# W behind four rows of x on the sync queue, the small loads alone on the scalar queue, and six transpositions of the identity at PE's start

## Chip, cores, metric

One core of one Trainium2 chip. The metric is the device time in microseconds of one execution (the slowest core, here the only one). The profile's span runs from the first to the last instruction and is about 1.3 us shorter than the time of the same execution. In the views PE, PEld (weight loads), DVE, ACT, POOL and SP are the engines, a q behind a name is that engine's sequencer, and `L213` is line 213 of the kernel.

## The reference

```python
x: [16, 2048, 256] f32 -> x_flat [32768, 256];  W: [256, 256];  lora_A: [256, 16];  lora_B: [16, 256];  lora_E: [16]
y = x_flat @ W + scale * (((x_flat @ lora_A) * lora_E) @ lora_B)
```

The kernel folds the low-rank part into the weights once: `weff = W + (A * E * scale) @ B`, and then does one product, `x_flat @ weff`. It must read 33.6 MB of x and write 33.6 MB of y.

## The kernel before

x is cut in 8 chunks of 4 MB. Six of them have a home in SBUF at a time; y is written over x in the same home, and a store sends it out. For each group of four rows per partition, POOL casts x to bf16 (`stage`), PE transposes it, ACT copies the result (`xt`), PE multiplies by `weff`, and DVE copies the product into the home. The parts that the argument touches:

```python
ROWS = 32; N_CHUNKS = 8; N_HOMES = 6
LOAD_PIECES = {0: [8, 8, 16]}            # chunk 0 is loaded in three pieces, the others in one of 4 MB
ORDER = ["L0", "L1", "L2", "L3", "L4", "L5",
         "S0", "S1", "L6", "L7", "S2", "S3", "S4", "S5", "S6", "S7"]
EARLY_AFTER = 1
HELD = N_HOMES - 1
...
    def sync_program():
        def load(pc):
            c, s, e = pc
            if c == N_HOMES - 1:
                sync.wait_ge(s_weff, 1)            # home 5 holds W until weff is made
            if c >= N_HOMES:
                sync.wait_ge(stored_of[c - N_HOMES], 16)
            ...
        opening.append(load(pieces[0]).ins.name)   # issued ahead of the entry barrier
        for step in ORDER:
            ...
                if c == EARLY_AFTER:               # the loads of chunk 2 and on wait for the first output
                    sync.wait_ge(s_first, 1)
                    sync.dma_start(out=y_chunks[0, :16, 0, :32], in_=home(0)[:16, 0, :32]).then_inc(s_early, 16)
            else:
                sync.wait_ge(s_chunk, c + 1)
                ...
                sync.dma_start(out=y_chunks[c], in_=home(c)[:]).then_inc(...)
...
    def gpsimd_program():
        ...
            if (c, b) == (HELD, 0):                # chunk 5 is not begun before stores 0 and 1 have landed
                for held_by in stored_of.values():
                    gpsimd.wait_ge(held_by, 16)
...
    def tensor_program():
        ...
        tensor.wait_ge(s_ident, 2)
        tensor.wait_ge(set_up_loaded["a"], 16)
        for t in range(KT):
            ins = tensor.transpose(psum_y[0][:R, t, :P], a_sb[:, t, :], ident[:])
        ...
        turn(0)
        ...   # (A*E)^T @ B
        turn(1)
        with tensor.Fori(0, N_GROUPS // UNROLL):
            for i in range(UNROLL):
                turn(i + 2)
                multiply(i)                        # so three groups are turned before the first product
```

## Time and profile before

| | before |
|---|---|
| time, median | 162.81 us (three runs, 162.21 to 162.82; with a fourth, 162.69) |
| span | 160.5 us (of a profiled execution of 161.79 us) |
| bytes moved | 67.43 MB |
| sync queue's packets, share of 16 DMA engines | 97.9% |
| last DVE copy ends / last store issued | 122.0 / 122.1 us |

The page of the kernel before, the 40-slice view (one digit is the busy tenths of a 4 us slice):

```profile
PE   0585979999999999400019999999990000000000
...
DVE  0102796999999999700003799899993000000000
...
DMA  7999999999999999999999999999999999999993
GB/s 262 432 425 466 449 393 425 490 392 408 498 400 392 492 400 400 400 417 466 425 400 451 457 392 433 474 402 425 466 400 433 466 408 433 449 425 417 441 449 155
```

and its DMA queues (packets, MB, share of 16 engines' span; q1 belongs to the sync queue, q10 to the scalar queue):

```profile
q1 hardware_dynamic: 2624, 67.11, 97.9%
q10 hardware_dynamic: 352, 0.30, 0.5%
```

The compute engines are idle for whole stretches; the DMA engines never are. The end of the chain of waits of the kernel before (start us, us, what), and from the view of waits of the sync queue its last wait (total us, times, longest):

```profile
120.74 0.02 issue
120.76 1.22 DVE home L213
```

```profile
SPq L264 <- SPq L264: 36.6, 1, 36.6
```

The chain ends with a DVE copy at 122 us because it follows instructions only. What comes after it is the sync engine waiting 36.6 us for stores that are already queued. That is the first thing to learn from these lines: the last instruction on a compute engine lies 38 us before the end.

The timeline of the kernel before in the head (start us, us, engine line op, names, shapes, count, idle before and what ended it):

```profile
0.00 2.44 SPq L131 DMA_DIRECT2D home<-in_x_dram  x4
...
1.99 0.53 ACTq L185 DMA_DIRECT2D home<-in_W_dram  x1
...
5.11 0.59 PE L248 MATMUL psum_y<-ident,home 128*16 128x128 f32 x2 [5.11 <-DMA home<-in_lora_A_dram]
...
12.95 0.69 DVE L208 TENSOR_TENSOR weff<-home,psum_y 128x512 bf16<-128x512 f32 x1 [5.91 <-DMA home<-in_W_dram]
...
13.79 1.86 PE L236 MATMUL psum_y<-weff,xt 128*128 128x256 bf16 x8 [2.48 <-PEq L221]
...
16.99 0.36 SPq L144 DMA_DIRECT2D out_dram<-home  x1
17.40 1.84 SPq L131 DMA_DIRECT2D home<-in_x_dram  x4
```

Here is what the change is aimed at: `weff` waited 5.9 us for W, and everything after it is late.

### The profile page before, as it was taken

The numbers are of one execution on the slowest core, as the hardware profiler recorded it, in microseconds if no ns is written. First come the engines' busy times: TensorE is split into PE (matmuls) and PEld (weight loads), VectorE is DVE, ScalarE is ACT, GpSimd is POOL, SyncE is SP. The second block draws the span as 40 slices with busy tenths as digits, with TensorE's granted clock in tenths as the row PEclk, the third lists the DMA queues.
The fourth block names the chain that finished last, engine by engine and source line by source line (L and its number), as shares of the span: only waits on it lengthen the run. The fifth ranks groups of instructions, "written<-read, shape, count | busy, mean of one in ns | idle before, by whom it ended". The sixth has DMA issues, their size and how long they took to land. (4 is left out here: it accounts for less than half of the span.)

```text
span 160.5 us, 2160 instructions
## 1 busy us (share of the span) xinstructions
PE 94.2 (59%) x782; PEld 83.9 (52%) x782; DVE 79.5 (50%) x66; ACT 66.0 (41%) x65; POOL 67.0 (42%) x70
## 2 busy tenths in 40 slices
PE   0585979999999999400019999999990000000000
PEld 0354869999999999300017999899990000000000
DVE  0102796999999999700003799899993000000000
ACT  3240667777777777400005577777740000000000
POOL 1542648777777777000045577777700000000000
PEclk9999999999999999955555999999998555555555
DMA  7999999999999999999999999999999999999993
GB/s 262 432 425 466 449 393 425 490 392 408 498 400 392 492 400 400 400 417 466 425 400 451 457 392 433 474 402 425 466 400 433 466 408 433 449 425 417 441 449 155
DMA packets 2979, 67.43 MB, mean 420 GB/s; under 512 B 528, under 2 KB 544, under 8 KB 672
## 3 DMA queue, kind: packets, MB, share of 16 engines
q1 hardware_dynamic: 2624, 67.11, 97.9%
q10 hardware_dynamic: 352, 0.30, 0.5%
q14 instruction: 3, 0.02, 0.0%
HBM read 33.85 MB, written 33.56 MB: 420 GB/s over the span
## 5 line engine op out<-in xcount | busy, mean ns | idle before, releaser
L213 DVE COPY home<-psum_y 128x1024 f32<-128x1024 f32 x64 | 78.3, 1225 | 30.0 <-PE psum_y L236 25.3
L173 POOL CAST stage<-home 128x1024 bf16<-128x1024 f32 x64 | 66.3, 1040 | 47.5 <-PE psum_xt L228 21.4
L193 ACT COPY xt<-psum_xt 128x1024 bf16<-128x1024 bf16 x64 | 64.7, 1012 | 49.8 <-PE psum_xt L228 49.8
L236 PE MATMUL psum_y<-weff,xt 128*128 128x256 bf16 x512 | 69.4, 281 | 2.6 <-PEq L221 2.5
L236 PEld LDWEIGHTS psum_y<-weff,xt 128*128 128x128 bf16 x512 | 51.4, 101 | 9.6 <-issue 3.2
L228 PE MATMUL psum_xt<-ident,stage 128*128 128x128 f32 x264 | 42.5, 287 | 18.6 <-PEq L221 18.6
L228 PEld LDWEIGHTS psum_xt<-ident,stage 128*128 128x128 f32 x264 | 33.1, 149 | 21.1 <-issue 20.2
L198 DVE TENSOR_SCALAR home<-psum_y,e_sb 16x256 f32<-16x256 f32 x1 | 0.5, 472 | 6.6 <-DMA e_sb<-in_lora_E_dram 6.6
L208 DVE TENSOR_TENSOR weff<-home,psum_y 128x512 bf16<-128x512 f32 x1 | 0.7, 689 | 5.9 <-DMA home<-in_W_dram 5.9
L248 PE MATMUL psum_y<-ident,home 128*16 128x128 f32 x2 | 0.6, 394 | 5.1 <-DMA home<-in_lora_A_dram 5.1
L248 PEld LDWEIGHTS psum_y<-ident,home 128*16 128x16 f32 x2 | 0.1, 87 | 5.1 <-issue 5.1
L193 ACT ACT_TABLE_LOAD x1 | 1.3, 1283 | 2.5 <-issue 2.5
L254 PE MATMUL psum_y<-home 16*128 16x256 f32 x4 | 2.1, 670 | 0.2 <-DMA home<-in_lora_B_dram 0.2
L254 PEld LDWEIGHTS psum_y<-home 16*128 16x128 f32 x4 | 1.2, 319 | 0.8 <-DMA home<-in_lora_B_dram 0.6
L152 POOL MEMSET ident<- 128x128 f32 x1 | 0.2, 204 | 0.7 <-SPq L268 0.7
L154 POOL TENSOR_SCALAR_AFFINE_SELECT ident<-ident 128x128 f32<-128x128 f32 x1 | 0.3, 292 | 0.2 <-POOL ident L152 0.2
L290 POOL MEMSET const-float32-0.0<- 128x1 f32 x1 | 0.1, 98 | 0.2 <-issue 0.2
L290 POOL MEMSET const-bfloat16-1.0<- 128x1 bf16 x1 | 0.1, 101 | 0.0
L290 POOL MEMSET const-uint8-127<- 128x1 uint8 x1 | 0.1, 101 | 0.0
L290 POOL MEMSET const-float32-1.0<- 128x1 f32 x1 | 0.1, 98 | 0.0
## 6 DMA issues: line engine op xcount, KB each, us to landing
out_dram<-home SPq DMA_DIRECT2D x8, 4096.0 KB, 39.7
home<-in_x_dram SPq DMA_DIRECT2D x7, 4096.0 KB, 20.8
home<-in_x_dram SPq DMA_DIRECT2D x2, 1024.0 KB, 5.7
home<-in_x_dram SPq DMA_DIRECT2D x1, 2048.0 KB, 11.5
home<-in_W_dram ACTq DMA_DIRECT2D x1, 256.0 KB, 10.9
home<-in_lora_A_dram ACTq DMA_DIRECT2D x1, 16.0 KB, 4.9
e_sb<-in_lora_E_dram ACTq DMA_DIRECT2D x1, 0.1 KB, 5.5
home<-in_lora_B_dram ACTq DMA_DIRECT2D x1, 16.0 KB, 5.8
```

Of the source, the lines that this page charges most:

```text
L152: gpsimd.memset(ident[:], 0.0).then_inc(s_ident, 1)
L154: gpsimd.affine_select(out=ident[:], in_=ident[:], compare_op=ALU.not_equal, fill=1.0, base=0, pattern=[[-1, P]], channel_multiplier=1,).t ...
L173: gpsimd.tensor_copy(out=stage[g % NS][:], in_=home(c)[:, b:b + CG, :]).then_inc(s_stage, 1)
L193: scalar.copy(out=xt[g % NX][:], in_=halves).then_inc(s_xt, 1)
L198: vector.tensor_scalar(out=ate, in0=psum_y[0][:R, :KT, :P], scalar1=e_sb[:], scalar2=float(scale), op0=ALU.mult, op1=ALU.mult,).then_inc(s ...
L208: vector.tensor_add(out=weff[:], in0=w_sb, in1=psum_y[1][:, :KT, :]).then_inc(s_free, NY)
L213: vector.tensor_copy(out=home(c)[:, b:b + CG, :], in_=psum_y[g % NY][:]).then_inc(s_free, 1)
L228: ins = tensor.transpose(psum_xt[i % NT][:, b, :], words[:, b, :], ident[:])
L236: ins = tensor.matmul(psum_y[i % NY][:, b, :], xt[i % NX][:, b, t, :], weff[:, t, :], start=(t == 0), stop=(t == KT - 1),)
L248: ins = tensor.transpose(psum_y[0][:R, t, :P], a_sb[:, t, :], ident[:])
L254: ins = tensor.matmul(psum_y[1][:, t, :], ate[:, t, :], b_sb, start=True, stop=True)
L290: nc = _bacc.Bacc("TRN2", target_bir_lowering=False, num_devices=1)
```

## The change

Intent: bring W early, so that `weff` and the first products come early; keep the scalar queue for the three small loads; let PE do something before A is there, so that its clock is released sooner; spread the early store over three lines.

```diff
-LOAD_PIECES = {0: [8, 8, 16]}
+LOAD_PIECES = {0: [4, 4, 8, 16]}
+WARM_UP = 6
+EARLY_LINES = [5, 6, 7]
...
         opening.append(load(pieces[0]).ins.name)
+        sync.dma_start(out=w_sb, in_=W.rearrange("(q t) m -> q t m", t=KT)).then_inc(set_up_loaded["w"], 16)
...
                     sync.wait_ge(s_first, 1)
-                    sync.dma_start(out=y_chunks[0, :16, 0, :32], in_=home(0)[:16, 0, :32]).then_inc(s_early, 16)
+                    for b, n in enumerate(EARLY_LINES):
+                        sync.dma_start(out=y_chunks[0, :n, b, :32], in_=home(0)[:n, b, :32]).then_inc(s_early, 16)
...
-                    sync.wait_ge(s_early, 16)
+                    sync.wait_ge(s_early, 16 * len(EARLY_LINES))
...
             ("b", b_sb, lora_B),
-            ("w", w_sb, W.rearrange("(q t) m -> q t m", t=KT)),
...
         tensor.wait_ge(s_ident, 2)
+        for i in range(WARM_UP):
+            tensor.transpose(psum_y[1][:, i % CG, :P], ident[:], ident[:])
         tensor.wait_ge(set_up_loaded["a"], 16)
```

## The prediction

> **What bounds it now.** The DMA engines, from first microsecond to last. In the 40-slice view DMA is 9 in every slice but the first (7) and last (3). In the DMA queue view the sync queue's packets fill 97.9% of 16 engines' span, the scalar queue's 0.5%. 67.43 MB move in a 160.5 us span. In the packet records of the trace a 32 KB packet takes 1.213 us (432 GB/s for 16 engines), so the bytes alone cost 156 us. The rest: first packet at 1.0 us, a slow first microsecond, about 0.7 us per engine at 55 to 65 us where loads give way to stores (packets of 1.5 to 1.8 us), and uneven finishing of the engines (158.1 to 160.0 us). PE is busy 59%, DVE 50%. The last DVE copy ends at 122 us (chain of waits), the last store is issued at 122.1, and 38 us of queued stores follow: compute has over 25 us of slack.
>
> **What the change does.**
> 1. W, issued on the scalar queue at 1.99 us, landed 10.9 us later; the weight sum began at 12.95 us after 5.9 us idle (timeline). W now goes out at about 1.1 us on the sync queue behind 512 KB of x, and should land near 4 to 5 us. The sum then waits for the small chain: A landed 5.1, E 6.6, B 7.3, B matmuls ended 9.4. I expect it at 9 to 10.5 us, the first main matmul near 10 (13.8 before).
> 2. Six transpositions of the identity: an estimate from the transposes at 6 us (272 ns each) is 1.6 us, at about 1.9 to 3.6 us, inside PE's wait for A, so free. The first clock record at 1.0 is at 17.4 us. The Trainium skill, "TensorE: Matmul & The Clock Gate", Part 1, says that about 3.4 us of activity releases the clock; six give half of that, so I expect little of them.
> 3. Smaller opening piece: one more issue (0.43 us of the sync queue). The second issue leaves at 1.1 us, its data follow about 1 us later, while the opening piece lasts until about 2.5 us: no DMA gap.
> 4. Three small early stores for one, 18 packets of 128 B for 16, at 13 ns each. The first chunk-2 load is issued at about 14 us, not 17.4; the queue holds work until 21.9, so neither time matters.
>
> **On the critical path: almost nothing.** The bytes are the same and the 16 engines are busy already. The Trainium skill, "DMA: Bandwidth & Descriptors", "Issuing engines are not separate DMA queues", says that queues share the 16 engines; this trace agrees (packets of both queues interleave, total share over 98%). Moving W reorders bytes. The 3 to 4 us won at the head go into slack: chunks 1 to 4 then wait for loads, chunk 5 is held until two stores land at 82 us, and the last store queues as before.
>
> **Predicted: 162.4 us, range 161.4 to 163.4.** Faster by over 2%: 2%; within 2%: 96%; slower by over 2%: 2%.
>
> **What would show it.** Right: DMA share still 97 to 99%, 420 GB/s; span 160 to 161 us; weight sum before 11 us; stores of chunks 0 and 1 landing near 72 and 82 us; last store issued near 122. Wrong: weight sum still waiting for W; a hole in DMA in the first 5 us; A's transposes late; last store issued later.
>
> **What would make it wrong.** If the early small stores change how the first real stores start (the 0.7 us at 58 us), or even out the engines' finish (up to 1.5 us), the time could fall by 1%; a DMA gap after the opening piece could add up to 0.5 us.

## The result and the profile after

| | before | after |
|---|---|---|
| time, median of four runs | 162.69 us (162.21 to 162.82) | 162.97 us (162.79 to 163.05) |
| span of the profile | 160.5 us | 161.6 us |
| `weff` begins | 12.95 us | 8.09 us |
| first product begins | 13.79 us | 11.85 us |
| loads of chunk 2 and on issued from | 17.40 us | 16.17 us |
| last store issued | 122.06 us | 122.78 us |

The ratio is 1.0021, 95% interval 0.9998 to 1.0044. A ratio is the mean time of one kernel's fast runs over that of the other's of the same rounds, so it is not quite the ratio of the medians quoted. The profile of before is of an execution of 161.79 us, quicker than its four timed runs, and that of the changed kernel of the one of 162.91 us: two profiles differ here by 1.1 us where the medians differ by 0.3.

The same views of the changed kernel, 40 slices:

```profile
PE   4858926999999999940009999999990000000000
...
DVE  0114750699999999970003799899993000000000
...
DMA  7999999999999999999999999999999999999993
GB/s 204 386 440 438 454 439 406 454 438 414 446 446 406 446 375 414 422 430 446 430 422 448 414 430 454 406 440 446 397 446 446 406 446 446 406 446 446 414 438 162
```

its DMA queues:

```profile
q1 hardware_dynamic: 2916, 67.37, 98.1%
q10 hardware_dynamic: 208, 0.03, 0.1%
```

the last wait of its sync queue:

```profile
SPq L269 <- SPq L269: 37.0, 1, 37.0
```

and its timeline in the head:

```profile
1.14 0.33 SPq L137 DMA_DIRECT2D home<-in_W_dram  x1
...
1.93 1.54 PE L250 MATMUL psum_y<-ident 128*128 128x128 f32 x6 [1.93 <-POOL ident L158]
...
3.84 0.60 PE L253 MATMUL psum_y<-ident,home 128*16 128x128 f32 x2 [0.37 <-DMA home<-in_lora_A_dram]
...
8.09 0.69 DVE L211 TENSOR_TENSOR weff<-home,psum_y 128x512 bf16<-128x512 f32 x1 [3.06 <-PE psum_y L259]
...
9.79 2.03 POOL L177 CAST stage<-home 128x1024 bf16<-128x1024 f32 x2 [1.45 <-DMA home<-in_x_dram]
...
11.85 1.91 PE L239 MATMUL psum_y<-weff,xt 128*128 128x256 bf16 x8
...
15.10 1.03 SPq L148 DMA_DIRECT2D out_dram<-home  x3
...
16.17 1.79 SPq L133 DMA_DIRECT2D home<-in_x_dram  x4
```

The wait for W is gone, and `weff` is 4.9 us earlier. The first product gains only 1.9 us, the first output 1.9 us, the end nothing. What got worse at the head is the GB/s of the first two slices: 204 and 386 where it was 262 and 432.

The windows view of both kernels for the head. The last two columns matter: share of the 16 DMA engines, and GB/s, both by packets that start in the window.

```profile
0.00:2.00 2.00, 0.00 (x0) 0.00 (x0) 0.00 (x0) 0.00 (x0) 0.70 (x6) 1.00 0.50 111
2.00:5.00 3.00, 0.00 (x0) 0.00 (x0) 0.00 (x0) 1.28 (x1) 0.16 (x1) 1.00 1.01 407
5.00:12.00 7.00, 5.64 (x18) 3.56 (x18) 0.47 (x1) 2.52 (x3) 3.94 (x4) 1.00 1.04 435
```

That is before; this is after:

```profile
0.00:2.00 2.00, 0.07 (x1) 0.08 (x2) 0.00 (x0) 0.01 (x1) 0.70 (x6) 1.00 0.45 82
2.00:5.00 3.00, 2.20 (x9) 1.34 (x10) 0.45 (x1) 1.27 (x1) 1.04 (x1) 1.00 0.97 325
5.00:12.00 7.00, 5.06 (x17) 3.42 (x18) 0.71 (x2) 2.02 (x2) 3.07 (x3) 1.00 1.02 415
```

Between 2 and 5 us the rate falls from 407 to 325 GB/s while the busy share falls by 0.04 only: a few engines stand idle, and some packets take longer than their size asks for. By the packet records 15.1 packets were in flight on the mean from 3 to 5 us (16.4 before; there are 16 engines, and records of one engine overlap a little), and the 4 KB packets of x that start between 2 and 5 us took 0.177 us on the mean, where their median over the whole run is 0.159.

### The profile page after: what moved, and what is told of

The parts are those of the page before. It is cut to its first block, busy times and chain, and to the rows that moved or that the text cites. A ratio compares the mean times of both kernels' runs of the same rounds, so it can differ in the third digit from the quotient of the medians.

```text
span 161.6 us, 2174 instructions
## 1 busy us (share of the span) xinstructions
PE 97.8 (60%) x788; PEld 86.4 (53%) x788; DVE 79.5 (49%) x66; ACT 66.1 (41%) x65; POOL 67.1 (42%) x70
## 3 DMA queue, kind: packets, MB, share of 16 engines
q1 hardware_dynamic: 2916, 67.37, 98.1%
## 5 line engine op out<-in xcount | busy, mean ns | idle before, releaser
L239 PE MATMUL psum_y<-weff,xt 128*128 128x256 bf16 x512 | 70.5, 283 | 0.1
L231 PE MATMUL psum_xt<-ident,stage 128*128 128x128 f32 x264 | 43.6, 292 | 21.3 <-PEq L224 21.3
L239 PEld LDWEIGHTS psum_y<-weff,xt 128*128 128x128 bf16 x512 | 52.1, 102 | 7.1 <-issue 0.3
L231 PEld LDWEIGHTS psum_xt<-ident,stage 128*128 128x128 f32 x264 | 33.7, 152 | 24.4 <-issue 23.6
L250 PE MATMUL psum_y<-ident 128*128 128x128 f32 x6 | 1.5, 430 | 1.9 <-POOL ident L158 1.9
L250 PEld LDWEIGHTS psum_y<-ident 128*128 128x128 f32 x6 | 1.1, 221 | 1.9 <-POOL ident L158 1.9
```

Source lines behind the costliest of these rows:

```text
L231: ins = tensor.transpose(psum_xt[i % NT][:, b, :], words[:, b, :], ident[:])
L239: ins = tensor.matmul(psum_y[i % NY][:, b, :], xt[i % NX][:, b, t, :], weff[:, t, :], start=(t == 0), stop=(t == KT - 1),)
L250: tensor.transpose(psum_y[1][:, i % CG, :P], ident[:], ident[:])
```

## The experiments

Theory S (slack): the DMA engines bound the kernel from start to end, the head is off that path, and its gain vanishes in slack. Beside it, a small loss comes from the pieces of 512 KB at the opening, which feed the DMA engines worse. Rivals: the loss comes from the three early stores or from W's place in the queue, or is noise; or the head does count and a loss elsewhere hides its gain.

Some figures below are worked out from the packet records of the traces. "Moved by 22 us" spreads each packet's bytes evenly over its duration and adds up. "Mean end" is the mean, over the 16 engines, of the start of the last completion packet, and "last end" the latest of them. "Excess" is the time of 32 KB packets above the usual 1.213 us, summed over a stretch and shared out over the 16 engines. Each is from one profile. The kernels of one call ran on one chip: `w_on_sync`, `pieces_only`, `early3_only` and `after_again` (before: median 161.82); `after_8_8_16`, `warm0`, `warm100` and `one_piece` (before: 162.07); `pieces_4x8` and `compute5` (before: 162.12); `warm100_no_gate` and `warm200` (before: 161.84).

| run | chunk 0 in | moved by 12 / 22 us, MB | mean / last end, us | time, median | ratio to before (95%) |
|---|---|---|---|---|---|
| before | 8, 8, 16 | 4.33 / 8.65 | 158.6 / 160.0 | see above | 1 |
| after (first profile) | 4, 4, 8, 16 | 3.94 / 8.27 | 159.6 / 161.2 | 162.97 | 1.0021 (0.9998 to 1.0044) |
| after_again | 4, 4, 8, 16 | 3.98 / 8.30 | 159.4 / 160.8 | 162.77 | 1.0042 (1.0002 to 1.0083) |
| w_on_sync | 8, 8, 16 | 4.22 / 8.55 | 158.7 / 160.5 | 162.01 | 0.9994 (0.9956 to 1.0033) |
| pieces_only | 4, 4, 8, 16 | 3.83 / 8.16 | 159.2 / 161.4 | 162.72 | 1.0023 (0.9981 to 1.0066) |
| early3_only | 8, 8, 16 | 4.05 / 8.38 | 158.8 / 160.0 | 162.29 | 1.0023 (0.9973 to 1.0072) |
| after_8_8_16 | 8, 8, 16 | 4.21 / 8.53 | 158.6 / 159.8 | 162.05 | 0.9993 (0.9968 to 1.0018) |
| warm0 | 4, 4, 8, 16 | 4.01 / 8.33 | 159.4 / 161.0 | 162.76 | 1.0037 (1.0011 to 1.0064) |
| pieces_4x8 | eight of 4 | 3.66 / 7.96 | 159.6 / 160.8 | 163.02 | 1.0054 (1.0023 to 1.0084) |
| one_piece | 32 | 4.32 / 8.63 | 158.5 / 160.5 | 162.59 | 1.0035 (1.0009 to 1.0062) |

One profile has scatter: before and `early3_only` have the same head (the early store comes at 17 us), and yet they differ by 0.27 MB at 22 us. So the groups of runs are compared, and the times decide.

### after_again: is the small loss real?

No edit; the changed kernel with more runs.

> The changed kernel once more, for an interval narrow enough to tell 0.2% from nothing. If the slower head is real: ratio 1.001 to 1.004 with the interval above 1.000; if the first figure was noise: 0.999 to 1.001.

Ratio 1.0042 with an interval just above 1 (1.0002 to 1.0083). By this run alone the loss is barely clear of noise; `warm0` below, which also has the small pieces, adds to it (1.0037, 1.0011 to 1.0064). The loss is about 0.2 to 0.4%.

### w_on_sync: W alone

```diff
+        sync.dma_start(out=w_sb, in_=W.rearrange("(q t) m -> q t m", t=KT)).then_inc(set_up_loaded["w"], 16)
-            ("w", w_sb, W.rearrange("(q t) m -> q t m", t=KT)),
```

> The kernel before with W alone moved to the sync queue (behind eight rows of x; pieces, early store and PE as before). Slack theory: the weight sum moves from 12.95 us to about 9 to 11 us, the time stays within 0.2 us of before (ratio 0.999 to 1.001), DMA share 97 to 99%. Rival (the head counts): 2 to 3 us faster (ratio 0.98 to 0.99). Theory of a slower head: if W's 2 KB packets in the queue of x are what cost the after kernel its 0.3 us, the ratio is about 1.002 and excess packet time or holes show between 2 and 12 us.

`weff` began at 9.43 us, as expected, and the first output was issued at 14.3 us, 2.7 us before the kernel before. The ratio is 0.9994 (0.9956 to 1.0033), which excludes the rival's 0.98 to 0.99: a head that is earlier by 2.7 us is worth nothing that can be seen, and 0.7 us at most. W in x's queue shows no cost either, but the interval would still hide one of the size in question; `after_8_8_16` below narrows that.

### pieces_only: the pieces alone

```diff
-LOAD_PIECES = {0: [8, 8, 16]}
+LOAD_PIECES = {0: [4, 4, 8, 16]}
```

> The kernel before with chunk 0 cut in [4, 4, 8, 16] rows and nothing else. Slack theory with a slower head: most of the 0.3 us loss of the after kernel is here (ratio 1.001 to 1.003), with holes of 0.1 to 0.7 us on some DMA engines between 2 and 5 us after the 512 KB opening piece, since the next piece is issued at 1.1 us and its data come late. Rival (the loss comes from the early stores or is noise): ratio 0.999 to 1.001 and no holes beyond those of before.

Its windows:

```profile
2.00:5.00 3.00, 0.77 (x3) 0.34 (x4) 0.00 (x0) 1.28 (x1) 1.04 (x1) 1.00 0.92 280
```

280 GB/s where before had 407. By the packet records, 12 to 14 packets were in flight between 3 and 5 us, where the kernel before had 16. The holes are there. They are not shared evenly: of the 16 completion updates of the second piece the first came at 4.58 and the last at 7.43 us (in before 7.27 and 7.69), and of those of chunk 1 still at 22.88 and 24.88 (22.30 and 22.77). So some engines fell about 2 us behind the first and stayed behind. One profile has scatter here too: at chunk 1 the spread is 1.0 to 2.0 us in the runs with [4, 4, 8, 16] and 0.5 to 1.2 in those with [8, 8, 16]. The ratio, 1.0023, has an interval that includes 1, so this run alone doesn't settle the time.

### early3_only: the three early stores alone

```diff
-                    sync.dma_start(out=y_chunks[0, :16, 0, :32], in_=home(0)[:16, 0, :32]).then_inc(s_early, 16)
+                    for b, n in enumerate([5, 6, 7]):
+                        sync.dma_start(out=y_chunks[0, :n, b, :32], in_=home(0)[:n, b, :32]).then_inc(s_early, 16)
```

> The kernel before with the one early store of 16 lines replaced by three of 5, 6 and 7 lines. Slack theory with a slower head: no change (ratio 0.999 to 1.001). Rival (the early stores cost time, by putting packets on seven of the 16 engines only or by leaving nine engines without an early store): ratio about 1.002, with the extra time at 55 to 65 us where loads give way to stores, or engines finishing less evenly than 158.1 to 160.0 us.

Ratio 1.0023 (0.9973 to 1.0072): unclear by itself. Nothing of what the rival expected shows in its profile: the excess packet time at 55 to 65 us was smaller than before (0.26 against 0.69 us per engine), and the last end 160.0 us as before. The next run settles the early stores.

### after_8_8_16: everything but the pieces

```diff
-LOAD_PIECES = {0: [4, 4, 8, 16]}
+LOAD_PIECES = {0: [8, 8, 16]}
```

(in the changed kernel)

> The changed kernel with chunk 0 cut in [8, 8, 16] again; W on the sync queue, six transpositions and three early stores stay. If the small pieces are what makes the changed kernel a little slower (holes of the DMA engines at 3 to 5 us, seen with the pieces alone): the rate over the first 5 us goes back from about 225 to about 270 GB/s, packets in flight stay near 16 of 16 engines, and the ratio is 0.998 to 1.002, below that of the changed kernel (1.002 and 1.004). If the early stores or W cost it: ratio stays 1.002 to 1.004.

Its windows:

```profile
2.00:5.00 3.00, 1.46 (x6) 1.06 (x6) 0.00 (x0) 1.27 (x1) 0.13 (x1) 1.00 1.01 381
5.00:12.00 7.00, 6.54 (x23) 4.25 (x24) 1.16 (x2) 2.74 (x3) 3.97 (x4) 1.00 1.04 431
```

The rate is back (381 and 431 GB/s), the mean end is at 158.6 us as before, and the ratio is 0.9993. All six runs (161.63 to 162.32) lie below all six of `warm0` on the same chip (162.43 to 163.15), which has the small pieces (and no transpositions; the changed kernel itself did not run on this chip). W's new place, the transpositions and the early stores together therefore cost nothing visible (the interval ends at 1.0018), and the small loss of the changed kernel is that of the pieces. `pieces_4x8` below, where the pieces alone are changed, says the same. This run even issued its first output earlier than the changed kernel, at 14.29 against 15.10 us (14.46 in the changed kernel's second profile); the reason is under point 1 below.

### warm0: no transpositions of the identity

```diff
-WARM_UP = 6
+WARM_UP = 0
```

(in the changed kernel)

> The changed kernel without the six transpositions of the identity. Slack theory: the time is that of the changed kernel within 0.2% (ratio to before 1.001 to 1.005), though the first main matmuls run cold longer (0.41 us each for the last of a group until about 17 us, where the changed kernel reached its 1.04 us groups at 14.3). Rival (a warm PE at the start counts): 1 to 2 us slower than the changed kernel.

Ratio 1.0037: the changed kernel's own. The first record of the full clock came at 13.6 us here, and at 14.2 and 15.6 us in the two profiles with six transpositions. So the six did nothing to the clock that can be seen either.

### warm100: the head late on purpose

```diff
-WARM_UP = 6
+WARM_UP = 100
```

(in the changed kernel)

> The changed kernel with 100 transpositions of the identity in place of six, so that A's transposes start near 18 to 20 us instead of 3.8 and everything in the head is late on purpose. Slack theory: only the part that runs past the queue's supply counts. The loads of chunk 2 wait for the first output, so they are issued near 25 us instead of 16.2, the queue runs dry at 22.5, and a DMA hole of 3 to 5 us opens; the time grows by that hole alone, to 165 to 168 us, not by the 15 us of delay. Rival (the head is on the critical path): about 177 us. Rival (PE time is all hidden behind DMA): 163 us.

The 100 took 13.0 us (0.13 us each, faster than I had put it), and ended at 14.9 us, 11.5 us after the six. A warm PE then caught up: the loads of chunk 2 were issued from 21.39 us, not near 25, which is 5.2 us later than in the changed kernel.

```profile
21.39 1.84 SPq L133 DMA_DIRECT2D home<-in_x_dram  x4
```

The expected hole of 3 to 5 us did not open. By the packet records 1.53 MB moved from 21 to 25 us, against 1.72 in the changed kernel and in before: 0.19 MB less, which is 0.4 us at 432 GB/s. Ratio 1.0109, 163.90 us, 1.1 us above `warm0` on the same chip. So about 11 us of delay at PE, 5 us of it left at the load issue, cost about 1 us, of which that shortfall is a part; where the rest went was not traced. The run also says something of the clock: its first full-clock record is at 5.8 us, after 3.9 us of transpositions alone.

### warm200: where the slack ends

```diff
-WARM_UP = 6
+WARM_UP = 200
```

(in the changed kernel)

> The changed kernel with 200 transpositions. By the run with 100, a transposition takes 0.13 us once warm, so everything in the head moves another 12 to 13 us: loads of chunk 2 issued near 34 us where the queue runs dry near 22.5, a DMA hole of about 12 us. Slack theory with that wait as the limit of the slack: every further microsecond counts now, time 175 to 178 us. If compute were hidden without limit: 164 us.

The windows of this run:

```profile
21.00:24.00 3.00, 3.00 (x30) 3.00 (x28) 0.00 (x0) 0.00 (x0) 0.00 (x0) 1.00 0.33 142
24.00:33.00 9.00, 8.70 (x73) 7.56 (x72) 3.83 (x5) 4.92 (x5) 5.10 (x5) 1.00 0.01 2
```

The DMA engines stand still (2 GB/s) from 24 to 33 us, since the loads of chunk 2 were issued only at 32.49 us.

```profile
32.49 2.03 SPq L133 DMA_DIRECT2D home<-in_x_dram  x4
```

That is 11.1 us later than with 100, and the time, 174.39 us, is 10.5 us longer. Now nearly every microsecond counts. The expected 175 to 178 was a little high: 0.13 us was a mean with the first, slower ones in it, and warm ones start 0.109 us apart. The slack of the head is therefore not that of the end (over 25 us): it runs until the queue is dry near 22.5 us, through the wait of chunk 2's loads for the first output.

### warm100_no_gate: the same delay without that wait

```diff
-                if c == EARLY_AFTER:
-                    sync.wait_ge(s_first, 1)
-                    for b, n in enumerate(EARLY_LINES):
-                        sync.dma_start(...).then_inc(s_early, 16)
...
-                if c == 0:
-                    sync.wait_ge(s_early, 16 * len(EARLY_LINES))
```

(in the kernel with 100 transpositions)

> The changed kernel with 100 transpositions of the identity, as before, but without the early stores and without the wait of the chunk 2 loads for the first output. Slack theory: the 11 us of delay in the head then cost nothing, the time is that of the changed kernel (ratio 1.002 to 1.005, the small pieces alone) and below the 1.011 of the same delay with that wait. If the delay itself is on the critical path: ratio 1.010 or more.

A miss, in part. The loads of chunks 2 to 4 now went out at once, and 442 GB/s flowed from 22 to 24 us, but the ratio is 1.0077 (1.0056 to 1.0099): above the changed kernel's 1.0021 to 1.0042 and not clearly below the 1.0109 (1.0077 to 1.0141) with the wait. In its profile the excess packet time where loads give way to stores (55 to 65 us) is 1.1 us per engine, the largest of any run; whether that belongs to the missing early store or to scatter was not tried. That the wait makes the slack end is shown by `warm200`; what the last 0.4% here are stays open.

### pieces_4x8: more small pieces

```diff
-LOAD_PIECES = {0: [8, 8, 16]}
+LOAD_PIECES = {0: [4, 4, 4, 4, 4, 4, 4, 4]}
```

> The kernel before with chunk 0 cut in eight loads of four rows (512 KB each) in place of [8, 8, 16]. Small-piece theory: every short load leaves the engines partly unfed, so the shortfall of the changed kernel (0.3 to 0.4 MB behind before at 12 us, worth 0.7 to 0.9 us) grows with their number: 0.8 MB or more behind at 12 us, ratio 1.005 to 1.015. If only the shortness of the very first load counts: 0.3 to 0.4 MB behind, ratio 1.002 to 1.004. If pieces do not matter: ratio 0.998 to 1.001.

0.67 MB behind at 12 us (0.8 or more was expected), 378 GB/s from 5 to 12 us against 435, and a ratio of 1.0054 whose interval excludes 1. More small loads, more shortfall: the direction of the small-piece theory, with the size at its lower edge. 0.69 MB at 22 us would be 1.6 us at 432 GB/s, and the median is only 0.9 us longer: the packets at 55 to 65 us had almost no excess in this profile (0.07 us per engine), so part seems to be given back there.

It is not the sync engine's issuing that limits. In `pieces_only` all 4 MB of chunk 0 had been issued by 2.5 us (issues at 0, 1.14, 1.52 and 2.0 us), while about 1 MB had moved by 5 us. Why short loads leave engines idle although work is issued, no run here shows.

### one_piece: one large piece, no wait

```diff
-LOAD_PIECES = {0: [8, 8, 16]}
+LOAD_PIECES = {}
-                if c == EARLY_AFTER: ...      # the wait and the early store, and the wait for it
```

> The kernel before with all of chunk 0 in one load of 4 MB and with no early store, so that no load waits for the first output (which would come only near 20 us). DMA theory: the largest packets from the start and no wait for the sync queue's issues; excess packet time at 2 to 12 us falls from 0.3 us per engine to under 0.1, ratio 0.994 to 0.999, though compute starts 6 us later (slack of 25 us). Rival (the early store is of use to the first real stores): excess at 55 to 65 us grows from 0.7 us per engine to well over 1 us, and the ratio is 1.000 or more. Rival (a late compute start costs): 2 us or more slower.

A miss on the time. The head carried no more than before (4.32 MB at 12 us), so [8, 8, 16] was already large enough, and the ratio is 1.0035. Neither did the first real stores suffer: the excess at 55 to 65 us was 0.33 us per engine. Why it is slower stays open. Its profile had moved as much as before by 150 us (63.73 against 63.67 MB), with the same mean end, and only the last engine ended later (160.5 against 160.0). The two runs without an early store, this one and `warm100_no_gate`, both came out slower than expected (1.0035 for 0.999 at most, 1.0077 for 1.005 at most). The kernel before without its early store alone was not tried, so it is not excluded that the early store is of use. What the run does show is the price of large packets to a small load on the other queue. The landing times of A (16 KB, on the scalar queue) in before, after and this run, from the view of DMA issues (KB each, us from issue to landing):

```profile
home<-in_lora_A_dram ACTq DMA_DIRECT2D x1, 16.0 KB, 4.9
```

```profile
home<-in_lora_A_dram ACTq DMA_DIRECT2D x1, 16.0 KB, 3.7
```

```profile
home<-in_lora_A_dram ACTq DMA_DIRECT2D x1, 16.0 KB, 12.3
```

A is 8 packets on each engine. They alternate with packets of x, which last 0.31 us (8 KB), 0.16 us (4 KB) or 1.21 us (32 KB): 8 x 0.31 = 2.5, 1.3 and 9.7 us, on top of a start near 2.5 us. The Trainium skill, "DMA: Bandwidth & Descriptors", "Queues, rings and completion order", says that an engine goes round its queue rows packet by packet; these three numbers agree, and in this run A's packets start in eight waves 1.2 us apart, from 2.9 us on. W itself landed 25.4 us after issue here.

### compute5: no compute in the last phase

```diff
-N_GROUPS = N_CHUNKS * GPC
+N_GROUPS = 5 * GPC
...
-                sync.wait_ge(s_chunk, c + 1)
+                if c < 5:
+                    sync.wait_ge(s_chunk, c + 1)
+                else:
+                    sync.wait_ge(loaded[(c, 0, ROWS)], 16)
```

(a wrong result; same bytes in the same order)

> A wrong result on purpose: the kernel before with only the first five chunks computed; chunks 5 to 7 are loaded and stored as they are, in the same order. All bytes move as before, but from about 66 us on no compute runs. DMA theory: the time falls by at most 1%, as compute is hidden. Straggler theory: in every trace so far one DMA engine alone runs 32 KB packets of 1.28 to 1.30 us (1.213 usual) while compute and stores overlap (at 62 to 69 and at 99 to 125 us), 15 to 27 of them, and it finishes 1 to 1.5 us after the mean of the engines; without compute after 66 us those at 99 to 125 us vanish, the last engine ends within 0.8 us of the mean, and the ratio is 0.991 to 0.996. Rival (that engine is slow in stores whatever runs): the slow packets stay, ratio 0.998 to 1.002.

Three eighths of the compute is gone and the ratio is 0.9973 (0.9928 to 1.0017): this part of the compute is worth at most 0.7% of the time. The slow packets (counted here as 1.27 to 1.34 us, from 62 us on) went from 19 to 7, and three of those seven lie at 99 us or later, where before had 18. That is as the straggler theory says. But the last end, 160.6 us, did not come earlier: the engine that ended last here had none of them but packets of 2.4 us (at 59.6) and 1.8 us (at 99.5), as far as its packets can be followed back from the end. So what makes one engine finish 1.1 to 2.1 us after the mean in every profile is not settled.

## Why the prediction was right, and where it was off

The time, 162.97 us, lies within the range, and "within 2%" holds. The direction was wrong: I put the change 0.4 us below the 162.81 us of before, and it came out 0.3 us above the four-run median. That the range held it is in part luck, as a range of 2 us hid a loss that was not in my sum. Of the signs of being right, the span (161.6 us for 160 to 161) and the landings of the first stores (73.6 and 83.2 us for 72 and 82) were missed by a little, and of the signs of being wrong a hole in the first 5 us did show.

**What bounds the kernel: right.** The DMA share is 98.1% after, the sync queue waits 37.0 us at the end (36.6 before), and the last store went out at 122.8 us. 13 us of PE work in the head (`warm100`) cost 1.1 us; three eighths of the compute less (`compute5`) gave at most 0.7%.

**Point 1, W: right in kind, two terms off.** W landed 3.7 us after its issue at 1.14 us, so at 4.8. The sum began at 8.09 us, before the predicted 9 to 10.5, because the small chain came sooner too: I kept the landings of A at 5.1 and of B at 7.3 us, and with packets of 4 KB between their own they landed at 3.8 and 5.6, so that the B matmuls began at 5.88 (7.34 before). The step that failed is "the first main matmul near 10": it was at 11.85. The prediction has it follow the sum directly, but PE's program turns three groups before the first product, and the third group is rows 8 to 11, which the cut [4, 4, 8, 16] brings with its third load. POOL's cast of it began only at 9.79 us, waiting for x. With [8, 8, 16] the second load brings it, and the first product was at 11.04 (`after_8_8_16`), although `weff` was later there (9.28):

```profile
11.04 1.91 PE L239 MATMUL psum_y<-weff,xt 128*128 128x256 bf16 x8
```

The other profiles of the small pieces with W moved have 11.21 (`after_again`) and 11.58 (`warm0`). So the small pieces delayed what they were to hasten, by 0.2 to 0.8 us, and near 10 was not reached with either cut.

**Point 2, the transpositions: right.** They ran from 1.93 to 3.47 us in the wait for A, and `warm0` shows no effect. The Trainium skill, "TensorE: Matmul & The Clock Gate", Part 1, gives about 3.4 us of activity for the release of the clock; `warm100` had 3.9 us of it before its first full-clock record and `warm200` 4.3, a little more than the page's figure, and six give 1.5 us.

**Point 3, "no DMA gap": this step failed.** The rate from 2 to 5 us fell from 407 to 325 GB/s. Over the runs, heads with [4, 4, 8, 16] had moved 8.16 to 8.33 MB by 22 us (`after`, `after_again`, `warm0`, `pieces_only`), heads with [8, 8, 16] 8.38 to 8.65 (`before`, `early3_only`, `after_8_8_16`, `w_on_sync`); `warm100_no_gate`, also with small pieces, lies between at 8.47. I had reckoned with issue times and one latency, and with full speed once work is queued. In this pair the bytes not moved in the head were not made up later: before had moved 0.38 MB more by 22 us and still 0.41 MB more by 150 us; the stores of chunks 0 and 1 landed at 73.6 and 83.2 us, a good microsecond after the 72.4 and 82.1 of before. In other profiles part was made up: `pieces_only` was 0.49 MB behind before at 22 us and 0.26 at 150, `pieces_4x8` 0.69 and 0.44, which fits their smaller excess at 55 to 65 us. 0.41 MB at 432 GB/s is 0.9 us. The medians of one call differ by 0.3 us (first call), 0.7 us (`warm0` and `after_8_8_16`) and 0.95 us (`after_again` and before), so the sum has the right order, and the exact size is not settled. I had named a gap here as a risk of up to 0.5 us. The Trainium skill, "DMA: Bandwidth & Descriptors", "Rules for kernel authors", asks for at least 1 MiB per transfer; the pieces of before are just that, those of the change half of it. I ought to have taken that line in.

**Point 4, the early stores: right** as far as the runs tell (`after_8_8_16` has them). The first load of chunk 2 was issued at 16.2 us, not 14, for the reason under point 1; as predicted, that did not matter.

**"The 3 to 4 us won at the head go into slack": right, with 1.9 us for 3 to 4.** `w_on_sync` and `after_8_8_16` win 2.7 us at the first output, and their ratios are 0.9994 and 0.9993. But "over 25 us of slack" is that of the last store only. The head has its own limit, the dry queue near 22.5 us (`warm100`, `warm200`).

No version tried beats the kernel before clearly. `after_8_8_16`, the change without its small pieces, equals it.

## What to carry to other kernels

Where the DMA queue never runs dry, an earlier start of compute is worth nothing that these runs could see, and a less well fed queue costs time (here 0.3 to 0.95 us between medians): look at the GB/s of the first slices before cutting the opening load smaller. Ask how many pieces the first product needs before choosing how to cut; here three groups had to be turned first, and a shorter first load moved the third group later. Slack has to be found for the place in question. At the head it is some 5 us (5.2 us later cost about 1 us, and nearly every microsecond after that counted). At the end an estimate is 27 us (the last wait of 36.6 us less 9.7 us for the last store's own 4 MB at 432 GB/s); no run delayed the end to test it.

## What the Trainium skill lacked or had wrong

- "TensorE: Matmul & The Clock Gate", Part 4, says that the full clock does not engage for transposes, as they do not count as PE activity in the same way. Here f32 transpositions (the program's `tensor.transpose`, which the trace lists as MATMUL) alone preceded its release: in `warm100` they began at 1.92 us, the first full-clock record is at 5.80 us, and single ones fell from 421 to 273 ns; in `warm200` the record is at 6.19 us.
- "DMA: Bandwidth & Descriptors": the rule of at least 1 MiB per transfer is there, but not that a run of shorter loads queued back to back leaves engines idle although the work was issued: 280 GB/s at 2 to 5 us with two pieces of 512 KB at the opening, against 407 with two of 1 MB.
- The same page has the round-robin between queue rows by packets, but not what follows for a small load beside a large one: 16 KB landed after 3.7, 4.9 or 12.3 us with packets of 4, 8 or 32 KB on the other queue.
- No page has the excess where a queue goes from loads to stores: in the profile of before, packets of 1.4 to 1.8 us in place of 1.213 and 0.7 us per engine at 55 to 65 us, with 0.07 to 1.1 us in the other runs (0.9 us at 70 to 75 us in `warm200`, whose stores begin later).
